# Moving the pools of a decoder trunk by a few hundred bytes, so that streamed and held matmul tiles begin 448 or 256 bytes apart

## The chip, the cores and the metric

The kernel runs on one core of one Trainium2 chip. The metric is the device time of the whole program in microseconds; lower is better. Where several runs of a kernel are given, their median counts. One core has a matrix engine (TensorE, PE in the profile), a vector engine (VectorE, DVE), an activation engine (ScalarE, ACT), a general one (GpSimd, POOL) and a queue processor (SyncE, SP) that here issues most of the DMAs. All of them read and write one on-chip memory of 128 partitions; an address in this document is the byte address within a partition, and it is the same in all of them.

## The reference

A decoder trunk for 512 tokens of width 1024: two layers, each of three sub-layers, six in all. Every sub-layer is `x = x + gate * f(norm(x) * (1 + scale) + shift)`, where shift, scale and gate come from a conditioning vector through one matrix per layer.

- Sub-layers 0, 2, 3 and 5 are SwiGLU feed-forwards: `(silu(h @ Wg) * (h @ Wu)) @ Wout`, 2816 wide, with a factor of one half.
- Sub-layer 1 is a gated short convolution: three projections, a product, a causal convolution of width 3, a product, an output projection.
- Sub-layer 4 is sparse attention: 16 heads in 4 groups, a compressed, a selected and a windowed branch with a shared relative-position bias, gated and summed, and an output projection.

Everything is float32.

## The kernel before, in words

**Layout and precision.** The activations are kept transposed, features in the partitions and tokens along the row: eight tiles `x0` to `x7` of 128 x 512. A float32 matrix product is made of three products in the faster fp32r form: every operand is split into a high part (`hi`, a rounded copy, ACT, L168) and a low part (`lo = src - hi`, DVE, L169), and `mm3` issues hi by hi (L172), hi by lo and lo by hi (L173, L174) into one PSUM tile. In the profile's names, `y<-ahi,whi` writes `y`, streams `ahi` past the array and holds `whi` in it. The *held* tile of a matmul (its weights, 128 columns) is loaded by PE's second sequencer (PEld) while the matmul before it still streams. So the pair of addresses that meet in time are the streamed tile of one matmul and the held tile of the next.

**Stages.** The six sub-layers follow each other as stages 0 to 5: `ffn_first`, `conv`, `ffn`, `ffn`, `nsa`, `ffn`. In the profiled execution they run from about 0, 400, 582, 930, 1280 and 1648 us. Each stage's norm starts while the matmuls of the stage before it (its *tail*, L339 adds them to `x`) are running, and the first weights of a stage are loaded and split ahead.

**ffn_first and conv.** These use matmuls with 512 columns: `hs` and `gu` are input projections from the normed activations `hhi`/`hlo`, `cv` the three projections of the convolution, `y` output projections from `ahi`/`alo` or `zhi`/`zlo`.

**ffn.** For each block of 128 hidden features, `seven_products` (L473 on) makes the two input projections with seven half-size products in place of eight, all with 256 columns. It needs sums of quarters of the weights: `qa` is loaded by SP (L489, L490) and a DMA issued by POOL adds a further quarter onto it (L492); `wraw` and `a22` are loaded by SP (L494, L495); DVE adds `qb` from `qa` and `wraw` (L496, L497); ACT and DVE split all of them into `whi`/`wlo`, `qah`/`qal`, `qbh`/`qbl`. On the streamed side it needs sums of token and feature blocks, `th` and `tl`, which are built from the norm (`hfull`, L313 on, the sums L320 to L328) before the first product. The output projections `y` have 512 columns; the last part's are `ty`, with 256. The first blocks of an ffn, `hs` and a first `gu`, use plain weights.

**nsa.** The input projections (`nat`) hold the activations and stream the weights; `s`, `pc`, `o` are the attention's own products; `ty` is its output projection.

**Where tiles lie.** Tiles come from pools, stacked from the left or from the right end of the memory (`side="right"`); a pool opened inside a stage takes the space that an earlier one has given back. The pools run through the whole program (`edge`, `cst`, `wp` with its three `whi`, `wlo`, `wraw` buffers, `tp`, `sp`) or a stage: `ada` (conditioning matrix tiles, and "own" weight tiles in stages 0 and 1), `hp` (the normed activations), `fa` in `Hidden` (`ahi`, `alo`), `tt` (`th`, `tl`), `swa` (`qa`, `qb`), `hw`, `sw`, `cva` and `tw` in `conv` (the convolution's streamed tiles, and the weights of its tail). The helper `shift(p, n)` (L62) puts a tile of `n` bytes that nobody uses first into a pool, so that all that follows lies `n` bytes further on. The kernel before has three of them: 32 bytes at the right edge, and 64 in `hw` and `sw`.

**What sets the order.** The kernel is written with a tile framework. It gives each tile its address, puts every instruction into its engine's queue in an order that it plans itself, and adds a wait wherever a tile, or a tile that earlier lay in the same bytes, is still in use. So addresses also decide waits: a load into a new tile waits for the last reader of each old tile under it, and a change of waits can change the planned order. Each engine works through its queue in order, so an instruction that waits holds up all behind it.

Two places where this matters here. When stage 2 begins, SP's first `qa` load (L489) goes to bytes that partly held a weight tile of `tw`, which the tail of `conv` reads to its end; POOL's adding DMA, DVE's `qb` add (L496) and the `hfull` rows behind it follow. Before stage 5, SP's queue holds the first `wraw` load of `seven_products` (L494) and then the `qa` loads; POOL's queue holds the adding DMAs, DVE's the `qb` adds, between instructions of the attention's tail and of the norm of stage 5.

Of the kernel before, what the change touches and what calls it, by code (L numbers as in the profile page):

```python
# [12 lines left out]
F32 = mybir.dt.float32  # L13
# [8 lines left out]
P = 128  # L22
# [30 lines left out]
def decoder_kernel(ctx, tc, xT, cT, ng, adaw, adab, ffi, ffo, cwi, cw, cwo,  # L53
# [3 lines left out]
    def pool(es, name, bufs, **kw):  # L57
        kw.setdefault("reuse_waits", "tile")
        return es.enter_context(tc.tile_pool(name=name, bufs=bufs, **kw))


    def shift(p, n):  # L62
        p.tile([P, n // 4], F32, name="shift")

    shift(pool(ctx, "edge", 1, side="right"), 32)
    cst = pool(ctx, "cst", 1)
    wp = pool(ctx, "wp", 4)
    tp = pool(ctx, "tp", 1)
# [7 lines left out]
    def psum(name, tag="mm"):  # L76
        tag = next(six) if tag == "mm" else {"pr": "o"}.get(tag, tag)
        return ps.tile([P, T], F32, name=name, tag=tag, bufs=2)
# [4 lines left out]
    def tmp(name, n=T, tag="t"):  # L83
        bufs, size = TAGS[tag]
        return tp.tile([P, n], F32, name=name, tag=tag, padded_shape=[P, size], bufs=bufs)


    ada_es = ctx.enter_context(ExitStack())
    ap = ada_es.enter_context(tc.tile_pool(name="ada", bufs=4))
    cond = ap.tile([P, D], F32, name="cond", bufs=1)  # L90
    x = [cst.tile([P, T], F32, name=f"x{d}") for d in range(KD)]
    ngs = cst.tile([P, NSUB * KD], F32, name="ngs")
# [20 lines left out]
    def mod(s, kind, d):  # L113
        c = s * NMOD + kind * KD + d
        return mods[:, c:c + 1]
# [72 lines left out]
    def project(o, w, wc, h, ks, first, last, a=0, b=T):  # L188
        c = slice(wc * P, (wc + 1) * P)
        for n, (kw, k) in enumerate(ks):  # L190
            mm3(o, w[0][:, kw, c], w[1][:, kw, c], h[0][k][:, a:b], h[1][k][:, a:b],
                first and n == 0, last and n == len(ks) - 1)
# [145 lines left out]
    def residual(s, d, o, nrm, a=0, b=T, late=False):  # L338
        nc.vector.scalar_tensor_tensor(x[d][:, a:b], o[:, 0:b - a], mod(s, 2, d), x[d][:, a:b], op0=ALU.mult, op1=ALU.add)  # L339
        if nrm is not None:  # L340
            nrm.square(d, a, b, late)
        elif b == T:
            nc.sync.dma_start(out[d], x[d])
# [30 lines left out]
    def spread(jobs, n):  # L374
        left, total = [n], len(jobs)

        def fill():
            left[0] -= 1
            while len(jobs) * n > total * left[0]:
                jobs.pop(0)()  # L380
        return fill


    def ffn_in(f, j, c, own=None):
        return weights(ffi[f, j, c], KD, P, own)


    def ffn_out(f, d, m, j0, j1, own=None):
        src = ffo[f, d:d + m, :, j0 * P:j1 * P].rearrange("d p c -> p d c")
        return weights(src, m * (j1 - j0), P, own)  # L390
# [20 lines left out]
    def pair(f, j, h, own=None, halves=False):  # L411
        gu = []
        for c in range(2):
            w = ffn_in(f, j, c, own if c else None)
            o = psum("gu")
            for a, b in HALVES if halves else ((0, T),):
                project(o[:, a:b], w, 0, h, [(k, k) for k in range(KD)], True, True, a, b)
            gu.append(o)
        return gu
# [3 lines left out]
    def ffn_first(s, f, nrm, nxt, extra, ahead, first, soon, own):  # L423
        with ExitStack() as es:
            hp = pool(es, "hp", 1)
            hid = Hidden(es, 18)
            h = nrm.alloc(hp)
            nj = FIRST
            early = spread(soon, PARTS[0][1] - nj)
            late = spread(extra, NJ - PARTS[0][1] + 2 * KD)  # L430

            def fill():
                early() if soon else late()

            js = [(j, c) for j in range(nj) for c in range(2)]
            w, os = [], [psum("hs") for _ in js]
            for d in range(KD):
                first(d)
                if d < len(js):
                    w.append(ffn_in(f, *js[d], own=own if d > 2 else None))  # L440
                nrm.whole(d)
                for n in range(len(w)):
                    for k in range(0 if n == d else d, d + 1):
                        project(os[n], w[n], 0, h, [(k, k)], k == 0, k == KD - 1)
            for j in range(nj):
                hid.activate(os[2 * j], os[2 * j + 1])
            for p, (j0, j1) in enumerate(PARTS):
                for j in range(max(j0, nj), j1):
                    hid.activate(*pair(f, j, h, own))
                    fill()  # L450
                n = j1 - j0
                a, ka = (hid.hi[j0:j1], hid.lo[j0:j1]), [(k, k) for k in range(n)]
                last = p == len(PARTS) - 1
                for d in range(KD - 3 if last else KD):
                    w = ffn_out(f, d, 1, j0, j1, own if d % 2 else None)
                    o = psum("y")
                    project(o, w, 0, a, ka, True, True)
                    if last:
                        residual(s, d, o, nxt)
                    else:  # L460
                        fill()
                        nc.vector.scalar_tensor_tensor(x[d], o, mod(s, 2, d), x[d], op0=ALU.mult, op1=ALU.add)
            assert not extra
            return tail(s, nxt, [(d, ffn_out(f, d, 1, j0, j1, own), 0, ka) for d in range(KD - 3, KD)], a, ahead)

    def ffn(s, f, nrm, nxt, w0, ahead):
        with ExitStack() as es:
            hp = pool(es, "hp", 1)
            hid = Hidden(es, 12)
            keep = hid.keep  # L470
            nj = 2
# [60 lines left out]
                keep(e[:, 0:2].rearrange("p a b -> p (a b)"))  # L532

            js = [(j, c) for j in range(nj) for c in range(2)]
            tt = pool(es, "tt", 1, side="right")
            swa = pool(es, "swa", 1, side="right")
            with ExitStack() as tf_es:
# [63 lines left out]
    def conv(s, nrm, nxt, extra, w0, ahead, own):  # L601
        with ExitStack() as es:
            h_es = es.enter_context(ExitStack())
            hp = pool(h_es, "hp", 1)
            ca = pool(es, "cva", 2, side="right")
            h = nrm.alloc(hp)
            ks = [(k, k) for k in range(KD)]
            zh, zl = [], []
            fill = spread(extra, 2 * KD - 3)
            for d in range(KD):  # L610
                if d == 0:
                    w = w0 + [weights(cwi[3], KD, P, own)]
                    *os, nx = head_start(nrm, h, [(lambda k, w=w_: (w, 0, k)) for w_ in w])
                else:
                    os = [nx] if d == 1 else []
                    for c in range(len(os), 3):
                        w = weights(cwi[3 * d + c], KD, P, own if (d + c) % 2 else None)
                        o = psum("cv")
                        project(o, w, 0, h, ks, True, True)
                        os.append(o)  # L620
                cg, v, b = os
                cs = tmp("cs")
                nc.scalar.activation(cs, cg, AF.Copy)
                u = ca.tile([P, T + 2], F32, name="u")
                nc.vector.memset(u[:, 0:2], 0.0)
                nc.vector.tensor_mul(u[:, 2:], cs, v)
                y = tmp("yc")
                nc.vector.tensor_scalar(y, u[:, 2:], cws[:, 2 * KD + d:2 * KD + d + 1], None, op0=ALU.mult)
                for i in (1, 0):
                    nc.vector.scalar_tensor_tensor(y, u[:, i:i + T], cws[:, i * KD + d:i * KD + d + 1], y,  # L630
                                                   op0=ALU.mult, op1=ALU.add)
                z = tmp("z")
                nc.vector.tensor_mul(z, y, b)
                hi = ca.tile([P, T], F32R, name="zhi", bufs=KD)
                lo = ca.tile([P, T], F32R, name="zlo", bufs=KD)
                split(z, hi, lo)
                zh.append(hi)
                zl.append(lo)
                fill()
            z = (zh, zl)  # L640
            h_es.close()
            tw = pool(es, "tw", 1, side="right")
            for d in range(KD - 3):
                w = weights(cwo[d], KD, P)
                o = psum("y")
                project(o, w, 0, z, ks, True, True)
                residual(s, d, o, nxt)
                fill()
            assert not extra
            return tail(s, nxt, [(d, weights(cwo[d], KD, P, tw), 0, ks) for d in range(KD - 3, KD)], z, ahead)  # L650
# [658 lines left out]
```

## Time and profile before

| | us |
|---|---|
| runs of the kernel before | 2007.16, 2012.41, 2017.42 |
| their median | 2012.41 |
| the profiled execution | 2003.76 |
| its span in the trace | 2002.0 |
| PE busy in it | 1929.8 |
| DVE busy | 1493.5 |
| ACT busy | 873.9 |
| POOL busy | 203.2 |
| mean granted TensorE clock | 0.992 of full speed |

The profiled execution is 8.65 us below the median of the runs. Durations and starts below come from its trace, and starts are counted from the beginning of its span. The profile lists groups of equal instructions with their count, the busy time of the group, the mean duration of one in ns, and, after a bar, the idle time of the engine just before them with what ended it. A matmul of 512 columns has a duration near 390 ns, one of 256 columns near 280 ns. Matmuls overlap: each starts before the one ahead of it has ended.

### The profile page before, as it was taken

The page shows a single profiled execution, that of the slowest core. Times are in us where ns is not written, and L with a number is a line of the kernel's source. Part 1 is how long each engine was busy: PE and PEld are TensorE (multiplying, and loading weights), DVE is VectorE, ACT ScalarE, POOL GpSimd, SP SyncE. Part 2 cuts the span into 40 slices and gives each one's busy share as a digit, 9 for nine tenths or more (in the row PEclk, how much of TensorE's full clock was granted, in tenths as well). Part 3 has the DMA queues.
Part 4 walks back from the last instruction along what each step waited for, and adds up shares of the span by engine and source line. Part 5 has one row for each costly group of instructions (what it writes and reads, how often), then busy time and mean ns, then how long its engine had stood idle before and what let it go on. Part 6 is the DMA issues. An engine that isn't in the chain of part 4 may idle for free.

```text
span 2002.0 us, 32444 instructions
## 1 busy us (share of the span) xinstructions
PE 1929.8 (96%) x12644; PEld 1745.2 (87%) x12644; DVE 1493.5 (75%) x2597; ACT 873.9 (44%) x1410; POOL 203.2 (10%) x279
## 2 busy tenths in 40 slices
PE   5999999999998999999999999999999899999999
PEld 3878888888897898999889899999888788898989
DVE  7888888674466686868769686886887977686865
ACT  3322222332244353434535343455778865343532
POOL 0000000100011000000000000001344530000000
PEclk9999999999998999999999999999999999999999
DMA  8889988422236564533656453143111224565621
GB/s 309 299 313 326 337 319 316 158 96 85 90 90 187 140 169 131 158 107 106 174 153 169 133 160 112 56 139 106 54 48 48 64 64 130 153 174 155 169 80 64
DMA packets 113046, 307.39 MB, mean 154 GB/s; under 512 B 13883, under 2 KB 14155, under 8 KB 112892
## 3 DMA queue, kind: packets, MB, share of 16 engines
q1 hardware_dynamic: 97164, 274.81, 40.0%
q0 software_dynamic: 15728, 30.51, 8.8%
q8 instruction: 99, 1.62, 0.3%
q14 instruction: 55, 0.45, 0.1%
HBM read 302.12 MB, written 3.15 MB: 152 GB/s over the span
## 4 chain that ended last, share of the span: by engine, by line
PE 78%; DVE 9%; DMA 5%; ACT 4%; issue 2%; SPq 1%; POOL 0%; DVEq 0%; ACTq 0%; POOLq 0%
PE gu L172 11%; PE gu L174 11%; PE gu L173 11%; PE y L172 7%; PE y L173 7%; PE y L174 7%; DMA adaraw<-in_adaw 2%; DVE wlo L169 2%; PE cv L172 2%; PE cv L173 2%; PE cv L174 2%; PE hs L172 2%; PE hs L173 2%; PE hs L174 2%; DMA qa<-in_ffi 2%
## 5 line engine op out<-in xcount | busy, mean ns | idle before, releaser
L168 ACT ACTIVATE whi<-wraw 128x1024 fp32r<-128x1024 f32 (+2 forms) x286 | 285.0, 1000 | 537.5 <-PE y L173 259.5
L169 DVE TENSOR_TENSOR wlo<-wraw,whi 128x1024 fp32r<-128x1024 f32 (+2 forms) x286 | 329.5, 1155 | 62.7 <-ACT whi L168 60.2
L172 PE MATMUL gu<-hhi,whi 128*128 128x256 f32 (+1 forms) x856 | 273.3, 319 | 5.9 <-ACT whi L168 5.9
L173 PE MATMUL gu<-hlo,whi 128*128 128x256 f32 (+1 forms) x856 | 272.8, 319 | 0.0
L174 PE MATMUL gu<-hhi,wlo 128*128 128x256 f32 (+1 forms) x856 | 271.6, 318 | 0.7 <-DVE wlo L169 0.7
L172 PE MATMUL y<-ahi,whi 128*128 128x512 f32 x587 | 230.0, 394 | 0.3 <-ACT ahi L168 0.3
L173 PE MATMUL y<-alo,whi 128*128 128x512 f32 x587 | 228.3, 391 | 0.4 <-DVE alo L169 0.4
L174 PE MATMUL y<-ahi,wlo 128*128 128x512 f32 x587 | 227.8, 391 | 0.0
L123 DVE CUSTOM_DVE_ANT_0 adaraw<-adaraw,cond 128x1024 f32<-128x1024 f32 x144 | 174.1, 1222 | 25.6 <-DMA adaraw<-in_adaw 24.1
L172 PEld LDWEIGHTS gu<-hhi,whi 128*128 128x128 f32 x856 | 161.4, 188 | 20.1 <-ACT whi L168 7.1
L174 PEld LDWEIGHTS gu<-hhi,wlo 128*128 128x128 f32 x856 | 161.0, 188 | 13.4 <-DVE wlo L169 1.1
L173 PEld LDWEIGHTS gu<-hlo,whi 128*128 128x128 f32 x856 | 161.4, 189 | 12.0
L492 POOL DMA_DIRECT2D qa<-in_ffi x57 | 68.6, 1204 | 822.3 <-DMA qa<-in_ffi 280.3
L172 PE MATMUL gu<-th,qah 128*128 128x256 f32 x456 | 128.5, 282 | 10.8 <-ACT p L519 10.8
L172 PEld LDWEIGHTS y<-ahi,whi 128*128 128x128 f32 x587 | 109.5, 188 | 27.8 <-ACT ahi L168 4.5
L173 PEld LDWEIGHTS y<-alo,whi 128*128 128x128 f32 x587 | 110.2, 188 | 25.3 <-DVE alo L169 2.5
L174 PEld LDWEIGHTS y<-ahi,wlo 128*128 128x128 f32 x587 | 110.2, 188 | 24.3
L172 PE MATMUL gu<-th,qbh 128*128 128x256 f32 x456 | 127.2, 279 | 3.1 <-ACT qbh L168 3.1
L563 DVE SCALAR_TENSOR_TENSOR x<-y,mods,x 128x512 f32<-128x512 f32 x72 | 54.0, 750 | 101.2 <-PE y L174 100.4
L173 PE MATMUL gu<-tl,qah 128*128 128x256 f32 x456 | 128.1, 281 | 0.0
L174 PE MATMUL gu<-th,qal 128*128 128x256 f32 x456 | 128.0, 281 | 0.0
L174 PE MATMUL gu<-th,qbl 128*128 128x256 f32 x456 | 127.2, 279 | 0.5 <-DVE qbl L169 0.5
(295 smaller groups left out, 5116.7 us busy)
## 6 DMA issues: line engine op xcount, KB each, us to landing
adaraw<-in_adaw SPq DMA_DIRECT2D x144, 512.0 KB, 5.9
wraw<-in_ffi SPq DMA_DIRECT2D x119, 512.0 KB, 3.7
qa<-in_ffi SPq DMA_DIRECT2D x114, 256.0 KB, 3.8
qa<-in_ffi POOLq DMA_DIRECT2D x57, 512.0 KB, 5.9
wraw<-in_ffo SPq DMA_DIRECT2D x72, 384.0 KB, 4.0
a<-in_ffi SPq DMA_DIRECT2D x57, 256.0 KB, 4.0
wraw<-in_cwi SPq DMA_DIRECT2D x24, 512.0 KB, 3.3
wraw<-in_nwi SPq DMA_DIRECT2D x20, 512.0 KB, 3.4
```

The costliest lines, as they stand in the source:

```text
L123: nc.vector.tensor_tensor_reduce(out=raw, in0=raw, in1=cond, scale=1.0, scalar=0.0, op0=ALU.mult, op1=ALU.add, accum_out=m)
L168: nc.scalar.activation(hi, src, AF.Copy)
L169: nc.vector.tensor_tensor(lo, src, hi, ALU.subtract)
L172: nc.tensor.matmul(o, sh, mh, start=first, stop=False)
L173: nc.tensor.matmul(o, sh, ml, start=False, stop=False)
L174: nc.tensor.matmul(o, sl, mh, start=False, stop=last)
L492: nc.gpsimd.dma_start(qa, bass.AP(tensor=a21.tensor, offset=a21.offset, ap=[a21.ap[0], [0, 2], a21.ap[1]]), accum_op=ALU.add)
L563: nc.vector.scalar_tensor_tensor(x[d], o, mod(s, 2, d), x[d], op0=ALU.mult, op1=ALU.add)
```

## The change

Only addresses are changed: no instruction is added or removed, and no size, loop or load. Five shifts are added or made larger. The one at the right edge grows from 32 to 96 bytes, which moves all pools of the right side 64 bytes down. `ada` gets a shift of 192 bytes, `hp` one of 256 bytes in `ffn_first` and `conv` and one of 128 in `ffn`, and a pool `gap` that holds 320 bytes and nothing else is put between `fa` and `tt` in `ffn`.

```diff
-    shift(pool(ctx, "edge", 1, side="right"), 32)
+    shift(pool(ctx, "edge", 1, side="right"), 96)
@@ the pool of the conditioning matrix, and of "own" weights
     ap = ada_es.enter_context(tc.tile_pool(name="ada", bufs=4))
+    ap.tile([P, 48], F32, name="shift", bufs=1)
     cond = ap.tile([P, D], F32, name="cond", bufs=1)
@@ def ffn_first
             hp = pool(es, "hp", 1)
+            shift(hp, 256)
             hid = Hidden(es, 18)
@@ def ffn
             hp = pool(es, "hp", 1)
+            shift(hp, 128)
             hid = Hidden(es, 12)
@@
             js = [(j, c) for j in range(nj) for c in range(2)]
+            shift(pool(es, "gap", 1, side="right"), 320)
             tt = pool(es, "tt", 1, side="right")
             swa = pool(es, "swa", 1, side="right")
@@ def conv
             hp = pool(h_es, "hp", 1)
+            shift(hp, 256)
             ca = pool(es, "cva", 2, side="right")
```

What this does to the distance from the start of a streamed tile to the start of the next matmul's held tile, modulo 512 bytes (a streamed tile that begins 448 bytes further on than the held one, modulo 512, is at distance 64):

| columns | distance | matmuls before | matmuls after |
|---|---|---|---|
| 512 | 0 | 1101 | 128 |
| 512 | 192 | 2442 | 49 |
| 512 | 256 | 23 | 3409 |
| 256 | 0 | 504 | 42 |
| 256 | 64 | 3623 | 5688 |
| 256 | 192 | 2643 | 456 |
| 256 | 256 | 122 | 601 |
| 256 | 320 | 694 | 785 |
| 256 | 448 | 375 | 389 |

The order of the matmuls is that of before, but for some 20 places around the start of stage 5. Waits change in two places, which the last part of the section on the kernel names: the first `qa` tile of stage 2 no longer lies over the tile of `tw` that is read last, and before stage 5 SP's queue has the `qa` loads ahead of the `wraw` load, and DVE's queue has the two `qb` adds some 60 places earlier.

## The prediction

> **What bounds the kernel now.** First the page's busy shares and its chain of work that ended last.
>
> ```profile
> span 2002.0 us, 32444 instructions
> PE 1929.8 (96%) x12644; PEld 1745.2 (87%) x12644; DVE 1493.5 (75%) x2597; ACT 873.9 (44%) x1410; POOL 203.2 (10%) x279
> PE 78%; DVE 9%; DMA 5%; ACT 4%; issue 2%; SPq 1%; POOL 0%; DVEq 0%; ACTq 0%; POOLq 0%
> ```
>
> TensorE (PE) is busy 96% of the span and holds 78% of the chain; matmuls are 128x512 (N=512) or mostly 128x256 (N=256). The whole time is therefore 12,644 pitches (start of one matmul to start of the next) plus some 72 us of gaps. The change moves no data and removes no work: it can act only through the pitch, if TensorE minds where its two operands lie, and through the waits, because tiles that used to overlap in memory no longer do, and the other way round. Next I read busy time by stretch, one from the conv stage and one from the ffn of stage 2.
>
> ```profile
> 450.00:500.00 50.00, 50.00 (x221) 41.24 (x220) 23.35 (x32) 12.58 (x15) 0.00 (x0) 1.00 0.25 85
> 700.00:750.00 50.00, 50.00 (x442) 50.00 (x441) 44.30 (x60) 25.65 (x36) 4.81 (x4) 1.00 0.62 169
> ```
>
> Columns: stretch, its length, then busy us and count for PE, weight load (PEld), DVE, ACT, POOL, then granted clock, DMA share, GB/s. In both PE is never idle, at clock 1.00: here only the pitch counts, about 226 ns (50 us / 221) for N=512 and 113 ns (50 / 442) for N=256.
>
> Does the pitch hang on addresses in the kernel before? Take the distance, modulo 512 bytes, from the start of a streamed tile to the start of the next matmul's held tile, and call it d; the pools' addresses give it. The change's "448 apart" is d = 64, its "256 apart" is d = 256. Grouped matmuls of four stretches, each of one d: d = 192 (535 to 560 us), d = 0 (152 to 157 us), N=256 with d = 64 (706 to 712 us), N=256 with d = 0 (387 to 391 us).
>
> ```profile
> L173 PE MATMUL y<-zlo,whi 128*128 128x512 f32 x36 | 14.2, 394 | 0.0
> L172 PE MATMUL y<-zhi,whi 128*128 128x512 f32 x36 | 14.1, 392 | 0.0
> L174 PE MATMUL y<-zhi,wlo 128*128 128x512 f32 x36 | 14.0, 388 | 0.0
> ```
> ```profile
> L172 PE MATMUL y<-ahi,whi 128*128 128x512 f32 x8 | 3.1, 389 | 0.0
> ```
> ```profile
> L172 PE MATMUL gu<-th,qah 128*128 128x256 f32 x8 | 2.2, 276 | 0.0
> ```
> ```profile
> L172 PE MATMUL ty<-ahi,whi 128*128 128x256 f32 x12 | 3.4, 283 | 0.0
> ```
>
> The last number before the second bar is the mean ns of one. Successive matmuls overlap, so a duration exceeds its pitch by a constant: 276 against the 113 above makes it about 163 ns. So yes: N=512 runs at 391.3 on average (394, 392, 388) with d = 192 and 389 with d = 0; N=256 at 276 with d = 64 and 283 with d = 0. Two floors follow. From 256 to 512 columns the duration grows by 389 - 276 = 113 ns, and 113 is also the whole pitch at 256: the stream alone takes 0.441 ns a column. So 389 and 276 are both about the stream's own rate, and an address can't go below it.
>
> **The change, part by part.** Placing the program's 12,600 matmuls in the order of the trace, with the addresses of before and after: at N=512, 2425 go from d = 192 to 256 and 990 from 0 to 256; at N=256, 2079 go from 192 to 64, 286 from 0 to 192, 430 from 192 to 256; 3614 stay at 64. Instructions and bytes moved are the same.
>
> *N=512.* d = 256 hardly occurs at N=512 in the trace (a dozen, in attention, where gaps drown it), so I bound it. Below: the floor, 389. Above: the dearest spacing at N=256 costs 283 - 276 = 7 ns, so 396. At 389: 2425 x (391.3 - 389) = -5.6 us and nothing for the 990. At 396: 2425 x 4.7 + 990 x 7 = +18.3 us. Each ns in between is 3.4 us. I take 389: the nearest row in kind is the multiple-of-256 spacing d = 0 at this same N, and 192 lies only 2 ns above it, so a whole 7 would be out of character here.
>
> *N=256, 192 to 64.* Whole-run groups (whi under gu is at 192, qah and qbh at 64, ehhi at 256 and 320):
>
> ```profile
> L173 PE MATMUL gu<-hlo,whi 128*128 128x256 f32 x552 | 153.8, 279 | 0.0
> L172 PE MATMUL gu<-th,qah 128*128 128x256 f32 x456 | 128.5, 282 | 10.8 <-ACT p L519 10.8
> L173 PE MATMUL gu<-hlo,qbh 128*128 128x256 f32 x228 | 63.1, 277 | 0.0
> L172 PE MATMUL ty<-ohi,ehhi 128*128 128x256 f32 x64 | 17.5, 282 | 0.0
> ```
>
> 192 stands at 279. 64 has groups on both sides of it, 277 and 282: it runs now at the 276 of the steady row above, now at some 281, and nothing here says which it will be. I take 1 ns, half of what the better group gains: 2079 x 1 = -2.1 us, between -6.2 (all at 276) and +6.2 (all at 282). *0 to 192:* 286 x (283 - 279) = -1.1, the 283 from the steady row. *192 to 256:* ehhi takes 282: 430 x 3 = +1.3, between -1.3 (276) and +1.7 (283). These three sum to -1.9.
>
> *The start of stage 2, an ffn (582 us).* Four views: SP's own wait, SP's and POOL's DMA issues, DVE, and the chain.
>
> ```profile
> SPq L489 <- PE ty L174: 15.9, 1, 15.9
> ```
> ```profile
> 581.34 0.33 SPq L489 DMA_DIRECT2D qa<-in_ffi  x1
> ```
> ```profile
> 585.66 1.26 POOL L492 DMA_DIRECT2D qa<-in_ffi  x1 [19.42 <-DVE rs_a L206]
> ```
> ```profile
> 591.05 0.69 DVE L496 TENSOR_TENSOR qb<-qa,wraw 128x512 f32<-128x512 f32 x1 [2.83 <-DMA qa<-in_ffi]
> 591.66 1.26 DVE L313 SCALAR_TENSOR_TENSOR hfull<-x,mods,pr 128x256 f32<-128x256 f32 x3
> ```
> ```profile
> 588.27 0.70 PE L262 MATMUL pr<-dg,ones 128*128 128x256 f32 x2
> ```
> ```profile
> 574.83 0.12 PE ty L173
> ...
> 585.66 5.37 DMA qa<-in_ffi
> ...
> 607.18 2.00 ACT whi L168 x2
> 609.22 0.58 PE gu L172
> ```
>
> The first qa tile lies over the last conv weight tile by 64 bytes, so SP's load waits 15.9 us, to the end of the conv tail's matmuls; POOL's accumulating DMA follows the load, and qb on DVE stands idle 2.83 us for it, with hfull queued behind. The new 320-byte gap moves qa off that tile, onto one whose last matmul is that at 574.83, 6.5 us before the load's 581.34: load, POOL's DMA and landing come some 6 us sooner, the landing near 585. qb then runs at 588.2, and the next late thing is pr (588.27 + 0.70 = 588.97): hfull starts near 589.15 instead of 591.66, 2.5 us earlier. The second tile's load still waits for the conv tail, until 581.34. What it is worth is read at PE:
>
> ```profile
> 608.27 0.39 PE L172 MATMUL gu<-hhi,whi 128*128 128x256 f32 x1 [3.83 <-ACT whi L168]
> ...
> 609.22 0.58 PE L172 MATMUL gu<-hhi,whi 128*128 128x256 f32 x1 [0.44 <-ACT whi L168]
> ...
> 612.02 0.41 PE L172 MATMUL gu<-hhi,whi 128*128 128x256 f32 x1
> ```
>
> The gap of 3.83 ends on the split of whi, which stands at the end of the chain from hfull; it falls by 2.5 to about 1.3. And after it some 13 matmuls run at 0.41 instead of 0.28, about 3.0 us where 13 x 0.113 = 1.5 would do, so 1.5 lost; a gap of 1.3 may not do that. Between 2.5 and 4.0 I take 3.5. By the Trainium skill ("TensorE: Matmul & The Clock Gate", Part 1: The HAM clock gate) an idle window of about 3.4 us halves TensorE's clock; the slow matmuls behind the 3.83 agree, and by the rule this part would be the full 4.0.
>
> *The start of stage 5, the last ffn (1648 us).* SP's order there changes: its four qa loads come ahead of the wraw load they stood behind, and on DVE the two qb adds move some 60 places forward, into the attention tail.
>
> ```profile
> 1631.95 0.33 SPq L494 DMA_DIRECT2D wraw<-in_ffi  x1
> 1632.39 0.37 SPq L489 DMA_DIRECT2D qa<-in_ffi  x1
> ```
> ```profile
> 1639.19 2.51 POOL L492 DMA_DIRECT2D qa<-in_ffi  x2 [17.88 <-PE ty L174]
> ```
> ```profile
> 1654.94 0.69 DVE L496 TENSOR_TENSOR qb<-qa,wraw 128x512 f32<-128x512 f32 x1
> ```
>
> ```profile
> 1624.32 0.22 PE L1087 MATMUL o<-pth,vn 128*128 128x128 f32 x1
> ```
> ```profile
> DMA to landing us min/median/max: 3.8/5.9/6.6
> ```
> ```profile
> L172 PE MATMUL gu<-hhi,whi 128*128 128x256 f32 x48 | 13.6, 284 | 1.2 <-ACT whi L168 1.2
> ```
> ```profile
> PE hs L173 <- DVE hlo L316: 0.4, 1, 0.4
> ```
>
> By their new waits the qa loads can go after the attention matmul at 1624.32, near 1625 instead of 1632.39; they land about 4 us later (the view of qa's landings, 3.8 at the least), POOL, idle 17.88 us, can issue at 1629, and its DMA lands by 1636, when DVE reaches qb; wraw, issued at 1631.95 still, lands then too. DVE does 1.4 us less (two adds of 0.69) where they stood, ahead of the last norm block, and 1.4 more in front of the tail's additions. PE waits only 1.2 + 0.4 us around there (the last two rows, a group and a wait), so I take -0.8, between -1.6 and +1.4.
>
> Sum: -5.6 - 1.9 - 3.5 - 0.8 = -11.8 us. Against the profiled execution (span 2002.0, run 2003.76) that is 1992.0. That run is 8.65 below the runs' median of 2012.41 (they spread over 10 us), and I carry the difference over to the median: 2000.6.
>
> **The rivals.** *Spacing 256 is dear (slower).* Place: every N=512 stream. At 396 the sum is +18.3 - 1.9 - 4.3 = +12.1: 2024.5. It decides from 392.5 ns on (389 + 11.8/3.4), where the sum is nil, and is slower by 0.5% from 395.4. For it: the 7 ns at N=256 with d = 0 shows that a multiple of 256 can be the worst distance, and ty<-ohi,ehhi at 282 is as slow. Against: at N=512 d = 0 is the best seen.
>
> *Spacing means nothing*, and the change does not do what it says: only the waits, -4.3: 2008.1. The Trainium skill (the same page, Part 2: What happens when you issue a matmul) gives TensorE two independent read ports, for streaming and for held operands, so the load of one should not disturb the other; by that the pitch terms vanish, and the sum is this rival's. Against: 388 to 394 beside a steady 389, and 276 beside 283, at one clock.
>
> *Given back.* PE's next gap in stage 2 waits on a chain of qa transfers; were its DMAs not tied to PE's progress, the 3.5 would come back as a longer gap: -8.3, 2004.1.
>
> ```profile
> 620.47 0.13 PE gu L174
> 622.52 6.06 DMA qa<-in_ffi
> 629.15 8.59 DMA qa<-in_ffi
> 640.41 0.28 ACT p L519
> ```
>
> The chain shows PE's matmul at 620.47 ahead of the first of these transfers, so it should move with PE.
>
> *DVE blocked ahead of stage 5.* If POOL's DMA there still lands near 1645 (1639.19 + 6), qb at 1636 would stop DVE for 9 us in the attention tail: up to +9 in place of -0.8, sum -2.0: 2010.4.
>
> **How the numbers follow.** A measurement of this kernel tells 0.5%, 10 us, from no change. Forecast 0.46 (2000.6, its own range 1993 to 2006, 0.26 of it beyond 0.5%); spacing dear 0.22 (half of it beyond +0.5%); spacing nothing 0.18; given back 0.07; DVE blocked 0.05; 0.02 for a faster stream. Faster 0.26 + 0.02 + 0.10 (runs' spread in the smaller gains) = 0.38; slower 0.11 + 0.03 for runs that scatter = 0.14; the rest, 0.48, within 0.5%. The range's low end, 1992, is the sum with the other terms at their gaining ends (64 at 276, -4.1 more; ehhi's spacing at the floor, -2.6; the two waits, -1.3); its high end, 2018, is spacing 256 at 394 ns. Left out are a stream below 389 and the upper half of the dear spacing.
>
> **What would show it.** Right: y groups at 389 in all three lines; gu<-hlo,whi at N=256 at 278 or less; no 2.83 wait on qb, the 3.83 gap under 1.5, no 0.41 rows behind it; qa loads near 1625 and no new DVE wait on qa. Wrong: y at 392 or more (from 393 slower), a gap at 640 longer than 5.2, or qb waiting in the attention tail.

## The result, and the profile after

The changed kernel takes 2024.32 us (median of 6 runs, 2016.77 to 2029.54) where the kernel before takes 2013.59 (6 runs, 2007.16 to 2017.42): ratio 1.0063, 95% interval 1.0041 to 1.0086 (the ratio is an estimate over the runs; the two medians alone lie 10.7 us apart). It is slower by 8 to 17 us; 2000.6 was forecast, and the result lies above the range.

The profiled execution took 2025.95 us, near its kernel's median. That of before, 2003.76, was one of the fastest of its kernel, 9.8 us below the median now known, so of the 22 us between the two spans about 11 lie in which executions were profiled, and not in the change. The page's first lines of after:

```profile
span 2024.0 us, 32447 instructions
PE 1944.1 (96%) x12644; PEld 1763.5 (87%) x12644; DVE 1494.2 (74%) x2597; ACT 874.1 (43%) x1410; POOL 203.0 (10%) x279
```

PE is busy 14 us longer for the same 12,644 matmuls, DVE, ACT and POOL as long as before. So the matmuls themselves got slower, though not those of 512 columns. Groups from 535 to 560 us, after (five lines added to the source move its line numbers by one to five: L172 to L174 of before are L173 to L175 here):

```profile
L173 PE MATMUL y<-zhi,whi 128*128 128x512 f32 x38 | 14.8, 389 | 0.0
L174 PE MATMUL y<-zlo,whi 128*128 128x512 f32 x37 | 14.4, 389 | 0.0
L175 PE MATMUL y<-zhi,wlo 128*128 128x512 f32 x37 | 14.4, 389 | 0.0
```

394, 392 and 388 have become 389, 389, 389: at 512 columns distance 256 is at the floor, as forecast. The 256-column groups of the whole run, after:

```profile
L174 PE MATMUL gu<-hlo,whi 128*128 128x256 f32 x552 | 155.0, 281 | 0.0
L174 PE MATMUL gu<-tl,qbh 128*128 128x256 f32 x456 | 128.0, 281 | 0.0
L174 PE MATMUL gu<-hlo,qbh 128*128 128x256 f32 x228 | 63.9, 280 | 0.0
L174 PE MATMUL ty<-alo,whi 128*128 128x256 f32 x138 | 39.3, 285 | 0.0
L174 PE MATMUL ty<-alo,th 128*128 128x256 f32 x96 | 26.5, 276 | 0.0
```

gu<-hlo,whi went from 279 to 281 when its distance went from 192 to the supposedly better 64. gu<-hlo,qbh, whose distance was 64 and is 64, went from 277 to 280. So the distance alone doesn't give the time. The two ty groups, which don't follow this pattern, went as forecast: the weights' from 280 to 285 (distance 192 to 256), those by th from 283 to 276 (0 to 192). How the slower products come about is seen in short windows of stage 2: of the kernel before, just behind a y phase (690 to 697 us), then at 700 to 705 and at 720 to 740, and of the changed kernel, at 720 to 740.

```profile
L173 PE MATMUL gu<-hlo,whi 128*128 128x256 f32 x8 | 2.2, 280 | 0.0
```
```profile
L173 PE MATMUL gu<-tl,qbh 128*128 128x256 f32 x6 | 1.7, 281 | 0.0
```
```profile
L173 PE MATMUL gu<-tl,qbh 128*128 128x256 f32 x20 | 5.5, 276 | 0.0
L173 PE MATMUL gu<-hlo,whi 128*128 128x256 f32 x16 | 4.4, 276 | 0.0
```
```profile
L174 PE MATMUL gu<-hlo,whi 128*128 128x256 f32 x17 | 4.8, 281 | 0.0
L174 PE MATMUL gu<-tl,qbh 128*128 128x256 f32 x16 | 4.5, 281 | 0.0
```

Before, all products start slow behind y, at 280 and 281, and all are fast some 13 us later, those at 192 and those at 64 alike. Seen matmul by matmul, the switch falls in that stretch on a turn of the distance: 23 products at 192, 60 at 64, 24 at 192, all slow, and fast from the second product at 64 on. After, where all have 64, the slow pitch holds from 689 us to the next y phase without a break.

The two changed waits did what their places said, with less gain and one loss. Start of stage 2, after, PE by time (the bracket is the idle time ahead) and PE's waits from 590 to 650 us, after and then before:

```profile
604.22 0.39 PE L173 MATMUL gu<-hhi,whi 128*128 128x256 f32 x1 [1.23 <-ACT whi L169]
...
605.17 0.39 PE L173 MATMUL gu<-hhi,whi 128*128 128x256 f32 x1 [0.45 <-ACT whi L169]
...
606.05 0.42 PE L173 MATMUL gu<-hhi,whi 128*128 128x256 f32 x1
...
608.62 0.40 PE L173 MATMUL gu<-hhi,whi 128*128 128x256 f32 x1
```
```profile
PE gu L173 <- ACT p L522: 5.4, 1, 5.4
PE gu L173 <- ACT whi L169: 1.7, 2, 1.2
PE gu L173 <- ACT qbh L169: 1.0, 1, 1.0
```
```profile
PE gu L172 <- ACT p L519: 5.2, 1, 5.2
PE gu L172 <- ACT whi L168: 4.3, 2, 3.8
PE gu L172 <- ACT qbh L168: 0.3, 1, 0.3
```

The gap fell from 3.83 to 1.23 (1.3 was forecast), but the two waits behind it grew by 0.9, and 13 matmuls still run at 0.4. Ahead of stage 5, after the change: SP's wraw load, the landing in the view of the wraw tile (1636 to 1655 us), DVE and PE:

```profile
1642.89 0.33 SPq L497 DMA_DIRECT2D wraw<-in_ffi  x1
```
```profile
DMA to landing us min/median/max: 7.4/7.4/7.4
```
```profile
1650.38 0.69 DVE L499 TENSOR_TENSOR qb<-qa,wraw 128x512 f32<-128x512 f32 x1 [3.37 <-issue]
```
```profile
1651.46 1.01 PE L255 MATMUL pr<-ones,nacc 128*128 128x1 f32 x4 [3.63 <-DVE nacc L238]
```

wraw lands at 1642.89 + 7.4 = 1650.3, and qb runs at once: DVE stood 3.4 us for it in the middle of the attention's tail, and PE 3.6 us for a sum of squares queued behind qb. In the same view of before (1615 to 1665 us) that load took less than half as long:

```profile
DMA to landing us min/median/max: 3.5/3.5/3.5
```

The gap is not all that was lost there. Behind it some 20 matmuls start 0.21 us apart in place of 0.11, at half the rate, which is about 2 us more. Groups of after, 1652.6 to 1656.5 us, and of the same product before, 1638 to 1645 us:

```profile
L173 PE MATMUL ty<-ohi,ehhi 128*128 128x256 f32 x6 | 2.5, 415 | 0.0
```
```profile
L172 PE MATMUL ty<-ohi,ehhi 128*128 128x256 f32 x18 | 5.1, 281 | 0.0
```

### The profile page after: what moved, and what is told of

Same layout as the page of the kernel before. It is cut to its first block, busy times and chain, and to the rows that moved or that the text cites. A ratio compares the mean times of both kernels' runs of the same rounds, so it can differ in the third digit from the quotient of the medians.

```text
span 2024.0 us, 32447 instructions
## 1 busy us (share of the span) xinstructions
PE 1944.1 (96%) x12644; PEld 1763.5 (87%) x12644; DVE 1494.2 (74%) x2597; ACT 874.1 (43%) x1410; POOL 203.0 (10%) x279
## 5 line engine op out<-in xcount | busy, mean ns | idle before, releaser
L173 PE MATMUL gu<-hhi,whi 128*128 128x256 f32 (+1 forms) x856 | 274.0, 320 | 3.5 <-ACT whi L169 3.5
L175 PE MATMUL gu<-hhi,wlo 128*128 128x256 f32 (+1 forms) x856 | 273.2, 320 | 0.8 <-DVE wlo L170 0.8
L174 PE MATMUL gu<-hlo,whi 128*128 128x256 f32 (+1 forms) x856 | 273.3, 319 | 0.0
L173 PE MATMUL y<-ahi,whi 128*128 128x512 f32 x587 | 228.3, 391 | 1.3 <-ACT ahi L169 1.1
L174 PE MATMUL y<-alo,whi 128*128 128x512 f32 x587 | 227.4, 390 | 0.4 <-DVE alo L170 0.4
L175 PE MATMUL y<-ahi,wlo 128*128 128x512 f32 x587 | 227.0, 389 | 0.0
L173 PEld LDWEIGHTS gu<-hhi,whi 128*128 128x128 f32 x856 | 161.4, 189 | 16.9 <-ACT whi L169 4.7
L175 PEld LDWEIGHTS gu<-hhi,wlo 128*128 128x128 f32 x856 | 162.8, 190 | 13.1 <-DVE wlo L170 1.4
L174 PEld LDWEIGHTS gu<-hlo,whi 128*128 128x128 f32 x856 | 161.4, 189 | 12.3
L173 PE MATMUL gu<-th,qah 128*128 128x256 f32 x456 | 130.9, 287 | 17.0 <-ACT p L522 17.0
L173 PEld LDWEIGHTS y<-ahi,whi 128*128 128x128 f32 x587 | 109.5, 188 | 28.1 <-ACT ahi L169 5.5
L174 PEld LDWEIGHTS y<-alo,whi 128*128 128x128 f32 x587 | 110.2, 188 | 24.8 <-DVE alo L170 2.5
L174 PE MATMUL gu<-tl,qah 128*128 128x256 f32 x456 | 130.3, 286 | 0.0
L175 PE MATMUL gu<-th,qal 128*128 128x256 f32 x456 | 130.2, 286 | 0.0
L173 PE MATMUL gu<-th,qbh 128*128 128x256 f32 x456 | 128.3, 281 | 1.9 <-ACT qbh L169 1.9
L175 PEld LDWEIGHTS y<-ahi,wlo 128*128 128x128 f32 x587 | 110.2, 188 | 22.7
L175 PE MATMUL gu<-th,qbl 128*128 128x256 f32 x456 | 128.2, 281 | 0.6 <-DVE qbl L170 0.6
L174 PE MATMUL gu<-tl,qbh 128*128 128x256 f32 x456 | 128.0, 281 | 0.0
```

Of the source, the lines that this page charges most:

```text
L173: nc.tensor.matmul(o, sh, mh, start=first, stop=False)
L174: nc.tensor.matmul(o, sh, ml, start=False, stop=False)
L175: nc.tensor.matmul(o, sl, mh, start=False, stop=last)
```

## The experiments

Two theories. *The lock:* at 256 columns the stream has two steady pitches, it leaves y in the slow one, and it stays there while the distance stays the same; the change made the distance uniform and so locked it. *The place:* the pitch depends on where within 512 bytes the two tiles begin (streamed 448 and held 0 good, 64 and 128 bad), whatever went before.

To follow the pitch through all runs I add up, from each trace, the start-to-start times of the matmuls that neither wait nor run at the halved rate, less the floor (113.3 ns at 256 columns, 226.7 at 512). The table gives these sums in us, then TensorE's wait for pr ahead of stage 5 and the ratio:

| kernel | distances of the products | 256 columns | 512 columns | pr wait | ratio to before |
|---|---|---|---|---|---|
| before | 192 / 64 | 13.8 | 6.7 | under 0.3 | 1 |
| after | 64 | 27.2 | 1.4 | 3.6 | 1.0063 |
| e1 | 192 | 30.9 | 6.9 | under 0.3 | 1.0063 |
| e2 | 64 / 192 | 14.0 | 1.6 | 3.6 | 0.999 |
| e3 | 192 / 64 | 13.8 | 7.5 | 3.7 | 1.0007 |
| e4 | 192 / 64 | 12.6 | 1.5 | 3.9 | 0.9988 |
| e10 | 320 / 64 | 29.4 | 1.5 | under 0.3 | 1.0031 |
| e11 | 320 / 192 | 14.0 | 1.7 | 0.3 | 0.9975 |

**e1, one distance of 192 in the kernel before.** Edit, in `ffn`:

```diff
-            shift(sw, 64)
+            shift(sw, 192)
```

> The kernel before with one address changed: the pool of qah, qal, qbh, qbl lies 128 bytes further on, so that the 256-column products of an ffn all run at distance 192 (streamed at 448, held at 128) where before they changed between 192 and 64. All queues and waits are those of before. Theory of the lock: at 64 and at 192 the stream has two steady pitches, 113.3 and 117.8 ns; it enters an ffn's products from the 512-column y in the slow one and leaves it only where the distance changes or TensorE has paused. Then, with one distance, the slow pitch holds from the end of each y to the next pause: gu<-th,qah, gu<-th,qbh and gu<-hhi,whi all at 280 to 282 ns, +8 to +14 us over before (ratio 1.004 to 1.007). Rival, the place: what counts is where in the 512 bytes the two tiles begin, whatever comes before. Then the pair 448 and 128 keeps its 56% of fast matmuls and gives it to the others too: gu<-th,qbh near 279.5, +3 to +4 us (1.002).

Measured: 2025.54 us, ratio 1.0063 (1.0041 to 1.0086). Groups of e1 from 700 to 740 us:

```profile
L173 PE MATMUL gu<-hlo,whi 128*128 128x256 f32 x33 | 9.2, 279 | 0.0
L173 PE MATMUL gu<-tl,qbh 128*128 128x256 f32 x32 | 8.9, 279 | 0.0
```

No address of hhi, hlo, whi or wlo was touched, yet gu<-hlo,whi no longer reaches 276: in this stretch 504 products in a row run at the slow pitch (117.8 ns from start to start; at 192 the duration then reads 279, at 64 281). One address, no wait and no order changed, and the loss is that of the whole change. The place falls: its forecast was 1.002.

**e2, two distances in the changed kernel.** The same edit, made to the changed kernel.

> The changed kernel with the same one address moved: qah to qbl 128 bytes further on, so that the plain and first products (hhi by whi) stay at distance 64, streamed at 64 and held at 128, and the others get 192. Queues and waits are those of the changed kernel. The lock: the distance changes twice in every block again, so the stream finds the fast pitch some 10 us into each stretch: gu<-hhi,whi, whose own addresses are unchanged, falls from 282 to 279 or 280, gu<-th,qbh from 281 to 278 or 279; -8 to -13 us against the changed kernel, about 2012 to 2016, level with before. The place: gu<-hhi,whi keeps 282, for its tiles lie where they lay; the time stays within 4 us of the changed kernel.

Measured: 2009.73 us, ratio to before 0.999 (0.9974 to 1.0005), 15 us below the changed kernel. Groups of e2 from 693 to 699 us, from 702 to 708 us, and of the whole run:

```profile
L173 PE MATMUL gu<-tl,qbh 128*128 128x256 f32 x8 | 2.2, 279 | 0.0
```
```profile
L173 PE MATMUL gu<-tl,qbh 128*128 128x256 f32 x8 | 2.2, 276 | 0.0
```
```profile
L173 PE MATMUL gu<-hlo,whi 128*128 128x256 f32 x552 | 153.1, 277 | 0.0
```

The first 83 products behind y are slow; with the turn from 192 to 64 the stream is fast, and it stays so. gu<-hlo,whi, at the very addresses at which it took 281, takes 277. The lock stands.

**e3, the waits alone.** Edit, in the kernel before; 512 bytes change no distance:

```diff
+            shift(pool(es, "gap", 1, side="right"), 512)
             tt = pool(es, "tt", 1, side="right")
```

> The kernel before with a gap of 512 bytes ahead of th and qa in ffn: every tile keeps its place within 512 bytes, so every distance is that of before, but the overlaps, waits and queue orders are those of the changed kernel (SP's first qa load of stage 2 earlier, qa ahead of wraw and qb 60 places earlier ahead of stage 5). If the waits do what the two traces show at these places: stage 2's 3.8 us gap near 1.4, and DVE blocked some 3.4 us at qb in the attention's tail with TensorE waiting 3.6 us at pr: -2 and +4, in all +2 us, ratio 1.000 to 1.002. If the waits carry the whole growth of the gaps between the two traces, 9 us, ratio 1.004 or more. The pitches should be those of before in either.

Measured: 2015.66 us, ratio 1.0007 (0.9989 to 1.0025); the pitches are those of before. Waits of DVE (1620 to 1660 us) and PE (1600 to 1670) in e3:

```profile
DVE qb L496 <- issue: 3.7, 1, 3.7
```
```profile
PE pr L254 <- DVE nacc L237: 3.7, 1, 3.7
```

The loss ahead of stage 5 comes with the new order alone, and so does the half rate behind it (17 matmuls here, in e2 and in e4; none in the kernel before, e1, e10 and e11, whose order is the old one). On the whole the waits cost 1.4 us by the ratio, with an interval that reaches from -2 to +5, and 4.4 by the medians: the second outcome, that they carry the whole growth of the gaps, falls.

**e4, the 512-column half alone.** Edit: edge, `ada` and `hp` in `ffn_first` and `conv` as in the change; in `ffn` no shift of `hp`, and `gap` at 448. Against the changed kernel, in `ffn` (`...` stands for the lines between):

```diff
             hp = pool(es, "hp", 1)
-            shift(hp, 128)
...
-            shift(pool(es, "gap", 1, side="right"), 320)
+            shift(pool(es, "gap", 1, side="right"), 448)
```

> The half of the change that concerns 512 columns: edge, ada and hp in ffn_first and conv as in the changed kernel, hp in ffn left as before and the gap at 448 bytes, so that y, cv and gu run at distance 256 but the 256-column products keep the distances and places of before (192 and 64 in turn; only ty changes). Waits and queues are the changed kernel's. The lock: y at 389 to 390 in all three lines (-5.6 us), gu<-hhi,whi and gu<-th,qbh at 279 as before, the waits +2: 2009 to 2011, ratio 0.997 to 0.999. The place says the same of the products. If the distance of y, 256 in place of 192, decides in which pitch the products start, they may be slower or faster by up to 10 us.

Measured: 2010.66 us, ratio 0.9988 (0.9969 to 1.0008): the half that was right is worth its 5 us in the pitches, and the waits ahead of stage 5 take 3.9 of them back (table). Groups of e4 from 690 to 696 us:

```profile
L173 PE MATMUL gu<-tl,qbh 128*128 128x256 f32 x8 | 2.2, 276 | 0.0
```

Here the first turn already, after the first 23 products behind y, lets the stream out. Behind y the products start slow all the same, so y's own distance (256 here, 192 before) doesn't decide that.

**e5, e6, e7: one distance of 128, 384, 320.** Edit: `shift` of `hp`, `gap` and `sw` in `ffn` of the changed kernel at 64, 384, 128 (e5), 320, 128, 384 (e6) and 384, 64, 320 (e7).

> The changed kernel with all 256-column products of an ffn at distance 128 (hhi, th at 0, held tiles at 128) in place of 64; y stays at 256, waits and queues are the changed kernel's. No run so far has 128 at 256 columns. The lock is a matter of any one distance held without a break, if 128 has two pitches as 64 and 192 have: then gu<-th,qbh 281 and about 2020 to 2028 for the one run. If 128 has one pitch only, it shows from the first product after y on: at 276 the run comes to about 2005 to 2012, at 283 to about 2028. Rival: it is an odd multiple of 64 that makes the pitch unsteady; then 128, a multiple of 128, is steady at one value.

> The same at distance 384 (hhi, th at 256, held at 128); SP's and DVE's order ahead of stage 5 is that of the kernel before. Mirror of 128: if the pitch hangs on how far the two lie apart either way, it gives the same as e5; the lock with two pitches 281 and 2018 to 2026, one fast pitch 276 and 2003 to 2010, one slow pitch 283 and some 2026.

> The same at distance 320 (hhi, th at 320, held at 128); SP's and DVE's order ahead of stage 5 is that of the kernel before. nat<-whi,hhi, at 320 for four fifths in the kernel before, has both pitches in one group (mean near 115.3 by start to start, 282 to 283 ns with its pauses). The lock: 320 is like 64 and 192, slow from each y on, gu<-th,qbh at 281, 2018 to 2026. Rival: the mixed group comes from its one fifth at 448, and 320 alone is steady: fast, 276 and 2003 to 2010.

One run each: 2035.6, 2036.5 and 2026.1 us, beside one of 2011.4 of the kernel before. The same group of e5, e6 and e7 from 710 to 740 us:

```profile
L173 PE MATMUL gu<-tl,qbh 128*128 128x256 f32 x24 | 6.8, 284 | 0.0
```
```profile
L173 PE MATMUL gu<-tl,qbh 128*128 128x256 f32 x24 | 6.8, 284 | 0.0
```
```profile
L173 PE MATMUL gu<-tl,qbh 128*128 128x256 f32 x24 | 6.7, 281 | 0.0
```

128 and 384 have one pitch, a slow one (119.5 ns), as 0 and 256 have; 320 has two, and locks in the slow one. So at 256 columns a multiple of 128 was slow in every trace here, an odd multiple of 64 may be either. The times of e5 and e6 came out 8 to 10 us above what was expected for one slow pitch; with one run each, the figures to go by are the pitches.

**e8, e9: 96 and 32.** Edit: the same three shifts at 96, 352, 96 (e8) and 160, 288, 32 (e9).

> The changed kernel with all 256-column products of an ffn at distance 96 (hhi, th at 32, held at 128). So far 0, 128, 256 and 384 run at about 119.6 ns start to start, 64, 192 and 320 at 113.3 or 117.8. If only the distance modulo 128 counts and the pitch changes smoothly, 96, between 64 and 128, lies between 114 and 120 (277 to 283 in the groups), and the run comes to 2015 to 2035. If 32 bytes off the 64 already take the two reads out of each other's way, 113.3 from y on: gu<-th,qbh at 276, 2000 to 2010. If 96 has two pitches too, the lock, 281 and 2020.

> The same at distance 32 (hhi, th at 96, held at 128), between 0 and 64: the mirror of 96 if only the distance modulo 128 counts. Same three outcomes: between 277 and 283; one fast pitch of 276 and 2000 to 2010; or two pitches and the lock at 281.

One run each: 2038.3 and 2022.1 us, beside a median of 2016.3 of the kernel before. Groups of e8 and e9 from 710 to 740 us:

```profile
L173 PE MATMUL gu<-tl,qbh 128*128 128x256 f32 x25 | 7.0, 281 | 0.0
```
```profile
L173 PE MATMUL gu<-tl,qbh 128*128 128x256 f32 x24 | 6.7, 281 | 0.0
```

Neither has a fast pitch (means 118.8 and 118.3 ns over the run): no single distance tried is fast by itself. The time of e8 lies 3 us above its range, that of e9 inside its own.

**e10, turns of 256.** Edit: `hp` in `ffn` at 384 and `gap` at 64 in the changed kernel (`sw` stays at 64). With these, SP's and DVE's order ahead of stage 5 is that of before.

> A version meant to beat both: y at 256 as in the changed kernel, plain products at distance 320 and the others at 64 in turn, the first qa load of stage 2 early, and SP's and DVE's order ahead of stage 5 that of the kernel before (no DVE stop at qb). The lock says that the turns let the stream out of the slow pitch: N=256 rows at 279 or less, -5.5 for y, -2 to -4 for stage 2, and nothing lost ahead of stage 5: 2000 to 2006, ratio 0.995 to 0.997 against the kernel before. If the turn from 320 to 64 (or back) is not one that lets it out, the products stay at 281 as in e7 and the time is some 2018 to 2024 (1.004 to 1.006).

Measured: 2022.25 us, ratio 1.0031 (1.0009 to 1.0053): the second outcome, which I had not thought the likely one. Groups of e10 from 727 to 743 us:

```profile
L173 PE MATMUL gu<-tl,qbh 128*128 128x256 f32 x16 | 4.5, 281 | 0.0
L173 PE MATMUL gu<-hlo,whi 128*128 128x256 f32 x9 | 2.5, 281 | 0.0
```

The distance turns twice in every block, and the stream stays slow. So not every turn lets it out.

**e11, turns of 128.** Edit: e10 with `sw` at 192 in place of 64.

> The kernel of e10 with qah to qbl 128 bytes further on, so that the products change between 320 and 192 in place of 320 and 64; nothing else differs, queues and waits are the same. In e10 the turns between 320 and 64, a step of 256, left the stream in the slow pitch; in e2, e4 and the kernel before, the turns between 192 and 64, a step of 128, let it out. If the lock is kept by the distance modulo 256 and any step of 128 (320 to 192 is one) breaks it: gu<-th,qbh and gu<-hhi,whi at 276 to 279 but for the first block behind each y, full-clock excess of the 256-column products about 13 us in place of 29, -12 to -16 us against e10, 2000 to 2009, ratio to before 0.994 to 0.998. If only the pair 192 and 64 itself does it: as e10, 281 and 1.002 to 1.005.

Measured: 2005.32 us (12 runs), ratio 0.9975 (0.9961 to 0.999). Groups of e11 from 697 to 703 us and from 707 to 713 us, and its wait for pr (PE, 1600 to 1670 us):

```profile
L173 PE MATMUL gu<-tl,qbh 128*128 128x256 f32 x8 | 2.2, 279 | 0.0
```
```profile
L173 PE MATMUL gu<-tl,qbh 128*128 128x256 f32 x8 | 2.2, 276 | 0.0
```
```profile
PE pr L254 <- DVE nacc L237: 0.3, 1, 0.3
```

Slow in the first block, fast from the turn back on: 320 and 192 act as 64 and 192 do, 320 and 64 as one distance. The size of the step is not the whole rule, though. I counted every turn between two rows of 16 or more 256-column matmuls, each row of one distance (64, 192 or 320), in the traces of the kernel before, e2, e3, e4, e11 (steps of 128) and e10 (steps of 256):

| turn | slow ahead of it | fast behind it |
|---|---|---|
| away from 192, to 64 or 320 | 77 | 57 |
| from 64 or 320 to 192 | 38 | 0 |
| between 320 and 64 | 91 | 0 |

A step of 128 towards 192 never ended the slow pitch. Only leaving 192 did, in three cases of four, whether the turn stood behind the 24 products of a block (before, e3, e4) or behind the 60 (e2, e11). No turn ended the fast pitch: all 394 that began fast stayed fast. The products of e10 don't have the distance 192 at all, so whether its turns fail by the step of 256 or for want of 192 is not settled. e11 beats both kernels: the changed kernel's 512 columns, the turns of the kernel before, and its order ahead of stage 5.

## Why the prediction was wrong

- *512 columns, -5.6 us:* right. The y lines from 535 to 560 us read 389, all three, and the sum over the trace fell by 5.3; the matmuls that went from 0 to 256 neither gained nor lost, as forecast.
- *256 columns, -1.9 us:* this step failed. It took the distance for the cause of the pitch, so that only the matmuls whose distance moved could change, and the 3614 that "stay at 64" were costed at nothing. The runs show instead that at 64, 192 and 320 the same matmul has two pitches, 113.3 and 117.8, and that which it has is carried over from the matmul before: slow out of y, fast once a turn away from 192 has freed it. The change removed the turns. The 256-column sum rose by 13.4 us (13.8 to 27.2): 11.3 of it among the matmuls that stay at 64, and 2.4 among those that went from 192 to 64, for which -2.1 was forecast; the two small groups came to -1.7 (0 to 192) and +1.6 (192 to 256), near their forecasts. The prediction saw the two pitches ("now at the 276 of the steady row above, now at some 281") and left the point at "nothing here says which". It also read 192 as one value, 279, where that group too is a mean of two, 280 behind y and 276 later. The trace of before did say which it will be: behind each y phase the products start slow (some do so behind a pause too), and in the stretch shown this ends at a turn. Its upper bound of +6.2 for the 2079 could not have caught it either.
- *The start of stage 2, -3.5 us:* the mechanism was right, gap 1.23 for 1.3; the size was not. The half-rate matmuls stayed, and the next waits took back 0.9: the gaps and half-rate losses of stage 2 together fell by 1.8 us. The rival "given back" was thus right in part. By the Trainium skill ("TensorE: Matmul & The Clock Gate", Part 1: The HAM clock gate) it takes an idle window of about 3.4 us to halve the clock; here the halved rate followed gaps of 1.23 and 0.45 us, as it followed 3.83 and 0.44 before, so the measurement decides against the rule as I used it.
- *The start of stage 5, -0.8 us:* wrong in sign. The rival "DVE blocked" happened, at 3.4 us in place of 9, and by another transfer: not qa but wraw, whose load took 7.4 us where the step had 3.5. It was issued behind the qa transfers of SP and POOL. In the four kernels with that order the load took 7.4 to 7.7 us (after, e2, e3, e4), in the four with wraw ahead of qa 3.5 to 3.7 (before, e1, e10, e11); that it shared their way to memory is likely, but was not tried by itself. The cost was 3.6 us of gap and 1.8 more in half-rate matmuls behind it, which the prediction's sum had no term for.
- *The sum:* -5.3 + 13.4 - 1.8 + 3.6 + 1.8 = +11.7 us by the two traces, and 8 to 17 measured.
- *"Spacing 256 is dear"*, the slower rival: its time, 2024.5, is what came out, by chance, for its mechanism is false. At 512 columns 256 is the floor.
- *"Spacing means nothing":* false as well. One pool moved by 128 bytes in e1 cost 0.63%. So the rule that the Trainium skill gives ("TensorE: Matmul & The Clock Gate", Part 2: What happens when you issue a matmul), two independent read ports for streamed and held operands, does not carry over to timing here. Whether the two reads themselves get in each other's way, no run shows.

## What to carry to other kernels

When groups of equal instructions have two durations in one profile, find out where the one changes into the other before pricing a change that touches them: a stream can have a history, and then its mean under the old order says nothing about the new one. Making a good spacing uniform can be worse than mixing two. And when a vanished wait lets transfers go early, see which load is now issued behind them: here that load landed 3.9 us later, and an engine waited for it.

## What the runs showed that I had not expected

- At 256 columns the pitch of fp32r matmuls is 113.3 or 117.8 ns at distances 64, 192 and 320, and 119.5 to 119.8 at 128, 256 and 384. At 512 columns it is the other way round: 226.9 at distance 256, 229.1 at 192.
- The slow pitch lasted through 504 matmuls in a row (e1). Turns away from 192 ended it, 57 times of 77, in e2, e3, e4, e11 and the kernel before; turns towards 192, and those between 320 and 64 (e10), never did. Why such a turn ends it, why not always, and why y always leaves the stream in the slow pitch, no run here tells; a phase between the load of held columns and the stream would fit and was not tested.
- TensorE ran at half rate behind gaps of 1.23 and 0.45 us in the changed kernel (the rows at 606.05 and 608.62), but not behind 1.19 and 0.45 us at the same place in e4. PE in e4 by time:

```profile
602.65 0.38 PE L172 MATMUL gu<-hhi,whi 128*128 128x256 f32 x1 [1.19 <-ACT whi L168]
...
603.60 0.39 PE L172 MATMUL gu<-hhi,whi 128*128 128x256 f32 x1 [0.45 <-ACT whi L168]
...
604.32 0.28 PE L172 MATMUL gu<-hhi,whi 128*128 128x256 f32 x1
```

Behind the gaps of 3.6 to 3.9 us ahead of stage 5 the rate fell each time (after, e2, e3, e4). So for the short gaps the length alone does not say whether the rate falls behind them; what else does, no run here tells.
